# Post-norm chains with the reciprocal norm in PSUM, and squares summed by TensorE, in a two-layer decoder step

## The chip, the cores and the metric

The kernel runs on one core of one Trainium2 chip. The metric is the device time of one execution in microseconds (us). The median of three runs of the kernel before is 2349.43 us (2349.2 to 2352.71).

## The reference

One inference step of a two-layer trunk for a prompt of 1024 tokens and a group of 8 x 4 sample tokens, with shared weights and a model width of 1024. Layer 0 runs a convolution branch and a sliding-window attention branch behind one input projection; layer 1 is a gated linear recurrence. What bears on this change is what stands around each layer: the input is normed before the first projection, and the output of the last projection is normed (the post-norm), scaled and added to the layer's input.

```python
def rms_norm(x, g):
    xf = x.astype(jnp.float32)
    y = xf * lax.rsqrt(jnp.mean(xf * xf, axis=-1, keepdims=True) + NORM_EPS)
    return (y * g.astype(jnp.float32)).astype(x.dtype)

def even_layer(x, pos, conv_buf, kv_cache, pre_g, post_g, w_in, w_out, conv_w, conv_b, ln_g, ln_b):
    h = rms_norm(x, pre_g)
    proj = jnp.einsum('ntd,de->nte', h, w_in)
    ...
    y = jnp.einsum('nte,ed->ntd', jnp.concatenate([ya, yb], axis=-1), w_out)
    return x + rms_norm(y, post_g), conv_new, k, v

def odd_layer(x, s0, lb, pre_g, post_g, w_in, w_out, g_norm):
    h = rms_norm(x, pre_g)
    proj = jnp.einsum('ntd,de->nte', h, w_in)
    ...
    y = jnp.einsum('nte,ed->ntd', o, w_out)
    return x + rms_norm(y, post_g), s_new
```

So between the layers a token's 1024 values pass through two norms: the post-norm of layer 0, whose sum of squares is over `y`, and, once the sum `x + rms_norm(y)` is there, the pre-norm of layer 1, whose sum of squares is over that sum. The last output is the post-norm of layer 1 with its residual.

## The kernel before

Activations lie transposed: a tile has 128 features on the partitions and tokens along the free axis, so the width of 1024 is eight tiles, `k` or `ct` from 0 to 7. The 1056 tokens (1024 prompt and 32 sample) are cut in three chunks of `CW` = 384, 384 and 288 columns, chunk `c` = 0, 1, 2. A projection multiplies a 128 x 128 block of weights with such a tile. Weights and activations are each split in a high and a low fp32r part (for weights `w_high`, `w_split`: a ScalarE cast and a subtract on VectorE or GpSimd; for activations `self.xh`, `self.xl`), and three matmuls per tile stand for the full product, 24 for a chunk of eight tiles.

The order of work is not written out by hand. Jobs of TensorE (`dense`) run in a fixed order; everything else is a thread, a list of steps (`Atom`), each with an engine and the keys of the steps that it follows. While TensorE's matmuls are recorded, a planner with its own clock per engine (`sides`, `ready`, `account`) puts a step into its engine's queue when the planner's clock says that its inputs are there. The queues themselves run in order, with semaphores: a step that waits holds up whatever stands behind it on its engine. All operations are recorded by one helper, so every row of the profile has its line, L157; tiles tell them apart. `b` is any buffer in SBUF, `c` a buffer kept for the whole run (among them `xh` and `xl`, the ones matrix and the parameters), and `d`, `x`, `o` are tiles in PSUM: three, four and one of them.

The output projection of a layer (`project`) runs in three lists of jobs: `ja` with one half of the input features, for chunks 0 and 1, `jb` with the other half for the same chunks, and `jc` with both halves for chunk 2, eight jobs of 48 matmuls. As a tile of the result leaves PSUM, `ev_sum` squares it on ScalarE and adds the squares over the tiles on VectorE. Before `jb` starts, `post` spawns a thread for each chunk, which runs as follows:

- `stat` (TensorE, ScalarE): a matmul of the summed squares with a matrix of 1/128 (called the ones matrix here) gives the mean over the partitions in every row; `rstd_of` makes Ln and then Exp of it, which is the reciprocal norm. It is written to a half buffer in SBUF, `R[1]`.
- `ldx` (SyncE): the layer's input tile is loaded, `PX` = 3 tiles ahead (all eight for the last chunk of layer 1).
- `res` (VectorE): `y` times the post-norm's weight times `R[1]`, in place.
- `sum_` (GpSimd or VectorE, as the planner's clocks say): plus the input.
- In layer 0 then `hi` (ScalarE) and `lo` (VectorE), the high and low part of the next layer's input, `sq` (a store of the tile on SyncE, and its square on ScalarE) and `acc` (GpSimd or VectorE): the squares are added up over the tiles. In layer 1 `sq` is the store of the output alone.
- In layer 0 last `norm` (TensorE, ScalarE): the sum of squares times the ones matrix, and the reciprocal norm of layer 1's input, `R1`, by which the results of layer 1's projections are scaled as they leave PSUM.

The dense jobs of layer 1 use `xh` and `xl` of a chunk as soon as its `lo` steps are there. The first three jobs of layer 1 are cut by chunk (`HEAD0` = 3): three jobs on chunk 0, three on chunk 1, three on chunk 2, in 3 x 24 matmuls each. A matmul against the ones matrix is plain fp32 and appears as two records.

## Time and profile before

| what | value |
|---|---|
| median of three runs | 2349.43 us |
| the profiled execution | 2347.8 us, span 2344.8 us |
| TensorE (PE) busy | 2256.7 us, 96% |
| VectorE (DVE) busy | 1615.1 us, 69% |
| ScalarE (ACT) busy | 1023.7 us, 44% |
| GpSimd (POOL) busy | 1065.2 us, 45% |
| granted TensorE clock, mean | 0.987 of full |

The page's first part gives each engine's busy time; its second cuts the span in 40 slices, with TensorE's busy share and granted clock as digits (9 is 90% or more). The part of the trace that belongs to the change lies near the middle, at about 1120 to 1240 us, where layer 0 ends and layer 1 begins, and at the end, from about 2270 us. The busy tables by stretch show how much of each stretch an engine worked, and the granted clock in it; the timelines show single instructions and, in brackets, how long the engine had stood before them and who released it.

### The profile page before, as it was taken

To read this page: it belongs to the slowest core of one execution; us is meant where nothing else is said; L and a number is where in the kernel's file an instruction comes from. 1 tells how busy PE (TensorE), PEld (TensorE's weight loads), DVE (VectorE), ACT (ScalarE), POOL (GpSimd) and SP (SyncE) were. 2 spreads that over 40 slices of the span, in tenths; PEclk is the share of its full clock that TensorE was granted. 3 is DMA by queue.
4 is the path that set the end of the run, shared out by engine and by line. 5 is a ranking of instruction groups with operands and counts; after the bars stand their busy time and mean duration, and the time that the engine had idled before them with its cause. 6 is when DMAs were issued, how large, how long until landed. Compare 5 with 4: busy or idle time off the path is not lost.

```text
span 2344.8 us, 42760 instructions
## 1 busy us (share of the span) xinstructions
PE 2256.7 (96%) x17387; PEld 2115.6 (90%) x17387; DVE 1615.1 (69%) x2465; ACT 1023.7 (44%) x1856; POOL 1065.2 (45%) x706
## 2 busy tenths in 40 slices
PE   7999999999989999999979999999999999999997
PEld 6988888898887788899969999999999999998996
DVE  7999899998885656732776666666666666667336
ACT  5454454444445323332455444444454444444332
POOL 4655465555464523543654333333333333344436
PEclk9999999999999999999979999999999999999998
DMA  4131221221246978862540212222112221132535
GB/s 152 56 96 40 61 93 49 69 76 49 70 154 247 346 288 310 288 216 96 165 149 30 73 68 71 71 72 74 50 62 72 72 72 66 65 104 91 178 101 173
DMA packets 118173, 271.60 MB, mean 116 GB/s; under 512 B 32336, under 2 KB 59472, under 8 KB 117968
## 3 DMA queue, kind: packets, MB, share of 16 engines
q1 hardware_dynamic: 117968, 268.78, 33.5%
q8 instruction: 139, 2.28, 0.4%
q14 instruction: 66, 0.54, 0.1%
HBM read 215.00 MB, written 53.73 MB: 115 GB/s over the span
## 4 chain that ended last, share of the span: by engine, by line
PE 63%; DVE 3%; DMA 2%; ACT 1%; POOL 1%; issue 1%; SPq 0%; POOLq 0%; DVEq 0%; ACTq 0%
PE d L157 33%; PE x L157 29%; DVE b L157 3%; ACT b L157 1%; DMA b<-vc 1%; POOL b L157 1%; DVE c L157 1%; DMA b<-ybd 1%; PE o L157 0%; DMA b<-kc 0%; SPq L157 0%; DMA b<-x1d 0%; ACT c L157 0%; POOL c L157 0%; ACT L157 0%
## 5 line engine op out<-in xcount | busy, mean ns | idle before, releaser
L157 PE MATMUL d<-c,b 128*128 128x384 f32 (+1 forms) x7920 | 1393.2, 330 | 20.5 <-ACT b L157 8.6
L157 PEld LDWEIGHTS d<-c,b 128*128 128x128 f32 x7920 | 1284.2, 189 | 67.9 <-issue 40.3
L157 POOL TENSOR_TENSOR b<-b,b 128x1024 fp32r<-128x1024 f32 (+7 forms) x423 | 854.1, 2031 | 827.5 <-ACT b L157 616.6
L157 ACT ACTIVATE b<-b 128x384 f32<-128x384 f32 (+14 forms) x647 | 356.8, 567 | 801.6 <-DVE b L157 783.2
L157 PE MATMUL x<-c,b 128*128 128x384 f32 (+4 forms) x3616 | 581.3, 311 | 3.7 <-DVE b L157 2.9
L157 PEld LDWEIGHTS x<-c,b 128*128 128x128 f32 (+2 forms) x3616 | 540.0, 175 | 18.5 <-issue 5.1
L157 DVE SCALAR_TENSOR_TENSOR b<-b,c,b 128x1024 f32<-128x1024 f32 (+2 forms) x258 | 410.2, 1593 | 10.7 <-ACT b L157 8.3
L157 DVE TENSOR_TENSOR b<-b,b 128x384 f32<-128x384 f32 (+13 forms) x296 | 312.7, 1072 | 85.7 <-ACT b L157 69.9
L157 PE MATMUL x<-b,b 128*32 128x128 f32 (+12 forms) x4528 | 281.0, 340 | 12.2 <-POOL b L157 10.7
L157 DVE SCALAR_TENSOR_TENSOR b<-b,b 128x384 f32<-128x384 f32 (+3 forms) x216 | 193.2, 898 | 111.4 <-ACT b L157 103.2
L157 PEld LDWEIGHTS x<-b,b 64*32 64x32 f32 (+3 forms) x4528 | 201.0, 128 | 62.5 <-issue 38.0
L157 DVE TENSOR_TENSOR b<-d,b 128x384 f32<-128x384 f32 (+3 forms) x279 | 140.3, 509 | 142.4 <-PE d L157 133.8
L157 ACT CAST b<-b 128x1024 fp32r<-128x1024 f32 (+3 forms) x264 | 224.1, 862 | 31.8 <-DMA b<-od 7.8
L157 DVE TENSOR_TENSOR b<-x,b 128x384 f32<-128x384 f32 (+3 forms) x161 | 81.7, 508 | 130.7 <-PE x L157 115.8
L157 DVE COPY b<-x 128x512 f32<-128x512 f32 (+6 forms) x217 | 101.5, 479 | 77.3 <-PE x L157 70.1
L157 POOL TENSOR_SCALAR b<-b 128x32 f32<-128x32 f32 x40 | 28.6, 714 | 272.8 <-DVE b L157 272.8
L157 ACT COPY b<-x 128x512 f32<-128x512 f32 (+4 forms) x176 | 86.0, 496 | 143.7 <-PE x L157 132.1
L157 ACT COPY b<-d 32x384 f32<-32x384 f32 (+2 forms) x211 | 94.3, 447 | 123.4 <-DVE b L157 78.4
L157 DVE CUSTOM_DVE_ANT_0 b<-x,b 128x128 f32<-128x128 f32 (+8 forms) x144 | 72.0, 533 | 38.5 <-PE x L157 35.7
L157 ACT ACTIVATE b<-b,c 128x512 f32<-128x512 f32 (+1 forms) x112 | 95.1, 874 | 2.9 <-DVE b L157 0.5
L157 POOL COPY b<-b 128x32 f32<-128x32 f32 (+1 forms) x105 | 59.0, 571 | 50.3 <-DVE b L157 48.5
L157 POOL TENSOR_TENSOR b<-b,c 128x248 f32<-128x248 f32 (+1 forms) x48 | 66.8, 1408 | 23.5 <-PE d L157 16.3
(59 smaller groups left out, 928.4 us busy)
## 6 DMA issues: line engine op xcount, KB each, us to landing
b<-wc SPq DMA_DIRECT2D x64, 512.0 KB, 4.2
b<-wab SPq DMA_DIRECT2D x56, 512.0 KB, 5.9
b<-kc SPq DMA_DIRECT2D x64, 448.0 KB, 6.5
b<-vc SPq DMA_DIRECT2D x64, 448.0 KB, 7.5
b<-woa SPq DMA_DIRECT2D x32, 512.0 KB, 4.3
b<-woc SPq DMA_DIRECT2D x32, 512.0 KB, 4.1
b<-yd SPq DMA_DIRECT2D x16, 528.0 KB, 6.4
ybd<-b SPq DMA_DIRECT2D x16, 512.0 KB, 3.0
```

The source lines that it names most:

```text
L157: r = f(*a, **k)
```

## The change

The reciprocal norm `R[1]` of the post-norm is written to the one PSUM tile `o` in place of a half buffer in SBUF, in both layers, so `res` reads one operand from SBUF and one from PSUM. Since there is one `o` tile, the statistic of chunk 1 or 2 gets a further condition: the last `res` of the chunk before.

In layer 0, for chunks 1 and 2 (`BYPE`), the step `acc` goes. TensorE sums over the partitions and over the tiles at once: `norm(0)` multiplies the squares of tiles 0 to 3 with the ones matrix into one PSUM tile, and ScalarE copies the result to a half buffer; `norm(1)` does tiles 4 to 7 into another, VectorE adds the two, and `rstd_of` follows. Chunk 0 keeps the adds and its single matmul (`norm1`). The claim of half buffers that must be free before a chunk's first load goes from `n + 4` to `n + 6`, and `R1` is taken before the three threads are spawned and no longer in chunk 0's last step.

```diff
--- before.py
+++ after.py
@@ -48,6 +48,7 @@
 PTAPS = 5
 QUEUE = 800
 HOLE = 700
+BYPE = (1,2)
 LAT = dict(pe=54.0, dve=33.0, act=33.0, pool=78.0)
 OVER = dict(dve=83.0, act=95.0, pool=54.0)
 
@@ -1619,7 +1620,7 @@
                 if two:
                     nc.tensor.matmul(p[:, :w], self.ones.f, self.last[:, :w], start=False, stop=True)
                     self.last.free()
-                R[key] = A.alloc(384)
+                R[key] = self.po()
                 self.rstd_of(R[key][:, :w], p[:, :w])
                 ss.free()
             return f
@@ -1639,8 +1640,6 @@
                 else:
                     nc.vector.scalar_tensor_tensor(y, y, self.P(P_POST, L * 8 + k), R[1][:, :w],
                                                    op0=OP.mult, op1=OP.mult)
-                if k == KT - 1:
-                    R[1].free()
             return f
 
         def sum_(k):
@@ -1683,22 +1682,37 @@
                     t.free()
             return f
 
-        def norm():
-            if c == 0:
-                self.R1 = A.alloc(NTOK)
+        def norm1():
             p = self.px()
             nc.tensor.matmul(p[:, :w], self.ones.f, R["ss2"][:, :w], start=True, stop=True)
             self.rstd_of(self.R1[:, cs], p[:, :w])
             R["ss2"].free()
 
+        def norm(half):
+            def f():
+                p = self.px()
+                for k in range(4 * half, 4 * half + 4):
+                    nc.tensor.matmul(p[:, :w], self.ones.f, R["t", k][:, :w], start=(k % 4 == 0), stop=(k % 4 == 3))
+                    R["t", k].free()
+                if half == 0:
+                    R["s"] = A.alloc(384)
+                    nc.scalar.copy(R["s"][:, :w], p[:, :w])
+                    return
+                s = R["s"][:, :w]
+                nc.vector.tensor_tensor(s, p[:, :w], s, op=OP.add)
+                self.rstd_of(self.R1[:, cs], s)
+                R["s"].free()
+            return f
+
         tag = ("post", L, c)
         K = lambda n, k: (tag, n, k)
         xs = [Atom(ldx(k), "sp", [("sum", L, c, 3)], K("x", k)) for k in range(KT)]
         n = PX if (L, c) != (1, 2) else KT
-        xs[0].claim = (0, n + 4)
+        xs[0].claim = (0, n + 6)
         atoms, xs = xs[:n], xs[n:]
-        atoms.append(Atom(stat(1), "pe", [("sum", L, c, KT - 1)], K("st", 1)))
-        fs = ([("dve", res), ("pool", sum_), ("act", hi), ("dve", lo), ("act", sq), ("dve", acc)] if L == 0 else
+        atoms.append(Atom(stat(1), "pe", [("sum", L, c, KT - 1)] + ([(("post", L, c - 1), 0, KT - 1)] if c else []),
+                          K("st", 1)))
+        fs = ([("dve", res), ("pool", sum_), ("act", hi), ("dve", lo), ("act", sq)] + [("dve", acc)] * (c not in BYPE) if L == 0 else
               [("dve", res), ("pool", sum_), ("sp", sq)])
         n = len(fs)
         for slot in range(KT + n - 1):
@@ -1711,8 +1725,11 @@
                     atoms.append(Atom(fs[st][1](k), fs[st][0], d, K(st, k)))
                     if st == 1 and xs:
                         atoms.append(xs.pop(0))
+                    if (L, st, k) == (0, 4, 3) and c in BYPE:
+                        atoms.append(Atom(norm(0), "pe", [K(4, 3)]))
         if L == 0:
-            atoms.append(Atom(norm, "pe", [K(5, KT - 1)], ("r1", c), (1, 0) if c == 0 else None))
+            atoms.append(Atom(norm(1), "pe", [K(4, KT - 1)], ("r1", c)) if c in BYPE else
+                         Atom(norm1, "pe", [K(5, KT - 1)], ("r1", c)))
         self.spawn(f"post{L}{c}", 0.01 * c, atoms, None, ("y", L, c))
 
 
@@ -2437,6 +2454,8 @@
             self.until(("ods", 1))
             for b in [self.cmask, self.rmask, self.qz] + self.smp1:
                 b.free()
+        if L == 0:
+            self.R1 = self.A.alloc(NTOK)
         for c in range(3):
             self.post(L, c)
         self.dense(jb)
```

The planner moves instructions in the two layers' ends and nowhere else. On TensorE, at the start of layer 1, before: two ones matmuls (the norm of chunk 0 from the sum `b1178`, the statistic of chunk 2 from `b1161`) within the first job on chunk 0, `d_12639`. `c4`, `c5`, `c12`, `c13` are `xh` and `xl` tiles, `c19` is the ones matrix, and `b1215`, `b1216` are the parts of the weights.

```order
L157 MATMUL d_12639<-c12_82,b1215_12539 128x384
L157 MATMUL d_12639<-c4_74,b1216_12540 128x384
L157 MATMUL x_12678<-b1178_12214,c19_89 128x384
L157 MATMUL x_12689<-b1161_12087,c19_89 128x288
L157 MATMUL d_12639<-c5_75,b1215_12539 128x384
L157 MATMUL d_12639<-c13_83,b1215_12539 128x384
L157 MATMUL d_12639<-c5_75,b1216_12540 128x384
```

After, the norm of chunk 0 and the statistic of chunk 1 stand in the first job on chunk 0; three jobs follow, and between them and the first job on chunk 1, `d_12802`, come the four squares of the first half of chunk 1:

```order
L158 MATMUL d_12712<-c8_78,b1227_12634 128x384
L158 MATMUL x_12776<-b1237_12732,c19_89 128x384
L158 MATMUL x_12776<-b1239_12750,c19_89 128x384
L158 MATMUL x_12776<-b1243_12767,c19_89 128x384
L158 MATMUL x_12776<-b1244_12774,c19_89 128x384
L158 MATMUL d_12802<-c1_71,b1212_12540 128x384
L158 MATMUL d_12802<-c9_79,b1212_12540 128x384
L158 MATMUL d_12802<-c1_71,b1213_12541 128x384
L158 MATMUL d_12802<-c2_72,b1212_12540 128x384
L158 MATMUL d_12802<-c10_80,b1212_12540 128x384
L158 MATMUL d_12802<-c2_72,b1213_12541 128x384
L158 MATMUL x_12812<-b1246_12788,c19_89 128x384
```

So the first ones matmul is followed by three more and by six matmuls of the job, and then by the second half, `x_12812`. Chunk 2's two halves stand in the same way, the first within the last job on chunk 1, the second within the first job on chunk 2. ScalarE's copy of the first half-sum stands in its queue before the `hi` steps of chunk 1's tiles 5 to 7, and likewise for chunk 2.

On VectorE, at the same place, before: the last steps of chunk 0 (`lo` into `c15` and `c16`, the adds of squares into `b1178`) between steps of chunk 1, whose `R[1]` is `b1156`.

```order
L157 TENSOR_SCALAR c20_90<-c17_87 128x1
L157 SCALAR_TENSOR_TENSOR b1049_10990<-b1049_10990,c17_87,b1156_12050 128x384
L157 SCALAR_TENSOR_TENSOR c9_79<-b1018_10701,c17_87,c1_71 128x384
L157 TENSOR_TENSOR b1178_12214<-b1178_12214,b1220_12582 128x384
L157 SCALAR_TENSOR_TENSOR c15_85<-b1099_11366,c17_87,c7_77 128x384
L157 SCALAR_TENSOR_TENSOR b1055_11108<-b1055_11108,c17_87,b1156_12050 128x384
L157 SCALAR_TENSOR_TENSOR c10_80<-b1035_10845,c17_87,c2_72 128x384
L157 SCALAR_TENSOR_TENSOR c16_86<-b1101_11396,c17_87,c8_78 128x384
L157 TENSOR_TENSOR b1178_12214<-b1178_12214,b1229_12650 128x384
L157 TENSOR_TENSOR b1227_12644<-b1217_12565,b1226_12643 128x1024
L157 SCALAR_TENSOR_TENSOR b1074_11211<-b1074_11211,c17_87,b1156_12050 128x384
L157 SCALAR_TENSOR_TENSOR c11_81<-b1049_10990,c17_87,c3_73 128x384
```

After: the two last adds of squares of chunk 0 (into `b1163`) stand before the evacuation of the eighth tile of chunk 2 (the copy from `d_12531`), and no step of chunk 1 stands in front of them.

```order
L158 SCALAR_TENSOR_TENSOR c16_86<-b1101_11396,c17_87,c8_78 128x384
L158 COPY b1099_11366<-d_12455 128x288
L158 TENSOR_TENSOR b1158_12079<-b1158_12079,b1210_12527 128x288
L158 TENSOR_TENSOR b1163_12114<-b1163_12114,b1207_12499 128x384
L158 TENSOR_TENSOR b1163_12114<-b1163_12114,b1214_12564 128x384
L158 COPY b1101_11396<-d_12531 128x288
L158 TENSOR_TENSOR b1158_12079<-b1158_12079,b1218_12597 128x288
```

What moved: all of chunk 1's steps went behind the layer-1 constants, and chunk 0's before them.

On VectorE at the end of layer 1, before: the last multiply of chunk 1 (by `b2144`) behind the evacuation of the eighth tile of chunk 2, `d_23398`.

```order
L157 TENSOR_TENSOR b2048_22046<-b2193_23308,b2048_22046 128x384
L157 SCALAR_TENSOR_TENSOR b2060_22133<-b2060_22133,c17_87,b2144_22925 128x384
L157 SCALAR_TENSOR_TENSOR b2087_22247<-b2087_22247,c17_87,b2144_22925 128x384
L157 TENSOR_SCALAR b2089_22277<-d_23398,c17_87 128x288
L157 SCALAR_TENSOR_TENSOR b2089_22277<-b2089_22277,c17_87,b2144_22925 128x384
L157 TENSOR_TENSOR b2005_21589<-b2005_21589,b2209_23490 128x288
L157 TENSOR_TENSOR b2012_21676<-b2012_21676,b2209_23490 128x288
```

After: the last multiply of chunk 1 (by `o_23273`) before the evacuation of the seventh tile, `x_23346`.

```order
L158 SCALAR_TENSOR_TENSOR b2059_22141<-b2059_22141,c17_87,o_23273 128x384
L158 SCALAR_TENSOR_TENSOR b2086_22255<-b2086_22255,c17_87,o_23273 128x384
L158 TENSOR_TENSOR b2086_22255<-b2194_23373,b2086_22255 128x384
L158 SCALAR_TENSOR_TENSOR b2088_22285<-b2088_22285,c17_87,o_23273 128x384
L158 TENSOR_SCALAR b2086_22255<-x_23346,c17_87 128x288
L158 TENSOR_TENSOR b2150_22980<-b2150_22980,b2196_23420 128x288
L158 TENSOR_SCALAR b2088_22285<-d_23425,c17_87 128x288
L158 TENSOR_TENSOR b2004_21597<-b2004_21597,o_23498 128x288
L158 TENSOR_TENSOR b2011_21684<-b2011_21684,o_23498 128x288
```

What moved: chunk 1's chain ends one job of chunk 2 earlier, and with it the stores of chunk 1, which stand on SyncE in front of the eight loads for chunk 2 in both kernels.

## Rows read from the trace of the kernel before

**Rows 1.** The page: busy share of TensorE, and its granted clock in 40 slices.
```profile
PE 2256.7 (96%) x17387; PEld 2115.6 (90%) x17387; DVE 1615.1 (69%) x2465; ACT 1023.7 (44%) x1856; POOL 1065.2 (45%) x706
PEclk9999999999999999999979999999999999999998
```
**Rows 2.** Busy table, seam: length, PE, PEld, DVE, ACT, POOL; clock, DMA share, GB/s.
```profile
1178.44:1238.06 59.62, 43.11 (x227) 40.86 (x225) 39.93 (x69) 33.80 (x60) 27.38 (x27) 0.80 0.38 126
...
1180.00:1190.00 10.00, 0.71 (x5) 0.39 (x3) 9.46 (x21) 4.45 (x9) 5.82 (x6) 0.63 0.84 283
1190.00:1200.00 10.00, 9.81 (x37) 8.92 (x38) 5.66 (x11) 5.00 (x11) 0.00 (x0) 0.68 0.27 88
...
1210.00:1220.00 10.00, 5.97 (x17) 5.36 (x18) 6.17 (x10) 4.50 (x8) 4.71 (x5) 0.50 0.26 83
```
**Rows 3.** Timeline of TensorE at the seam: start, us, work, [idle before, releaser].
```profile
1178.44 2.27 PE L157 MATMUL d<-c,b 128*128 128x384 f32 x12
1190.19 2.61 PE L157 MATMUL x<-b,c 128*128 128x384 f32 x4 [9.47 <-DVE b L157]
1192.18 4.37 PE L157 MATMUL d<-c,b 128*128 128x384 f32 x12
...
1214.03 1.65 PE L157 MATMUL x<-b,c 128*128 128x384 f32 x2 [7.04 <-DVE b L157]
1214.91 4.62 PE L157 MATMUL d<-c,b 128*128 128x384 f32 x12
...
1238.06 7.26 PE L157 MATMUL d<-c,b 128*128 128x384 f32 x41
```
**Rows 4.** Chain that ended last, two stretches of the output projection: start, us, work.
```profile
1113.15 4.16 PE x L157 x24
...
1146.81 6.33 PE x L157 x48
```
**Rows 5.** Timeline of TensorE, three ones matmuls in a row at full clock.
```profile
717.51 1.94 PE L157 MATMUL x<-b,c 128*128 128x384 f32 x6
719.38 0.66 PE L157 MATMUL o<-b,b 128*64 128x128 f32 x8
```
**Rows 6.** Instructions by shape, 1120 to 1245: busy us, mean ns; idle before.
```profile
L157 POOL TENSOR_TENSOR b<-b,b 128x384 f32<-128x384 f32 x21 | 28.3, 1358 | 20.5 <-DVE b L157 18.6 <-ACT b L157 1.8
L157 DVE SCALAR_TENSOR_TENSOR b<-b,c,b 128x384 f32<-128x384 f32 x16 | 20.8, 1305 | 1.1 <-ACT b L157 1.1
L157 ACT ACTIVATE b<-b 128x384 f32<-128x384 f32 x27 | 13.6, 518 | 13.4 <-DVE b L157 13.2
L157 ACT ACT_TABLE_LOAD x6 | 7.7, 1283 | 0.1
L157 DVE TENSOR_TENSOR b<-d,b 128x384 f32<-128x384 f32 x6 | 3.3, 552 | 12.0 <-PE d L157 12.0
```
**Rows 7.** Timeline of VectorE at the seam.
```profile
1182.93 0.61 DVE L157 SCALAR_TENSOR_TENSOR b<-b,c,b 128x384 f32<-128x384 f32 x1
...
1197.13 0.55 DVE L157 TENSOR_TENSOR b<-b,b 128x384 f32<-128x384 f32 x1
...
1211.94 1.57 DVE L157 SCALAR_TENSOR_TENSOR c<-b,c,c 128x288 fp32r<-128x288 f32 x2
```
**Rows 8.** Busy table of TensorE alone, in layer 0: length, busy, clock, DMA, GB/s.
```profile
973.60:977.00 3.40, 0.88 (x3) 1.00 0.83 306
977.00:980.40 3.40, 3.40 (x17) 0.63 0.02 7
```
**Rows 9.** Timeline of all engines at the kernel's end.
```profile
2328.50 1.77 DVE L157 TENSOR_TENSOR b<-b,b 128x288 f32<-128x288 f32 x3 [0.35 <-ACT b L157]
2329.63 3.76 SPq L157 DMA_DIRECT2D b<-x1d  x8
...
2333.66 4.23 DVE L157 TENSOR_TENSOR b<-b,b 128x288 f32<-128x288 f32 x8 [3.38 <-DMA b<-x1d]
...
2337.96 0.79 POOL L157 TENSOR_TENSOR b<-b,b 128x288 f32<-128x288 f32 x1 [0.76 <-DVE b L157]
```

## The prediction

> **What bounds the kernel now.** I read the page first, then the busy table of the seam between the two layers, then TensorE's timeline there, then the instructions by shape, and last the timeline of the kernel's end. TensorE is busy for 96% of the span and its clock row is at nine tenths or more nearly everywhere [rows 1], so a change can pay only where TensorE stands or runs slowly, or behind its last matmul. The seam is the largest such place. From the first matmul of layer 1 at 1178.44 to the first one after its chunk-by-chunk jobs at 1238.06 lie 59.62 us, of which TensorE is busy for 43.11, at a mean clock of 0.80 [rows 2, 3]. It stands twice, 9.47 and 7.04 us, each time at a matmul against the ones tile and each time released by VectorE [rows 3]: the first is the next norm of chunk 0, the second that of chunk 1, and both wait for the sum of squares that VectorE and GpSimd add up tile by tile.
>
> The other loss is the clock. [...] Check of the sum: the seam's matmuls need six times 24 at 384 columns, 0.1733 each (4.16 for 24), and three times 24 at 288 columns, 0.132 each (6.33 for 48) [rows 4], 34.5 us; plus four against the ones tile, which at full clock are 0.64 us for 384 columns and at three quarters of that, 0.49, for 288: six records, that is three matmuls of 384, 384 and 288 columns, stand from 717.51 to 719.38 [rows 5], 1.87 us where these two prices give 1.77. That makes 2 x 0.64 + 2 x 0.49 = 2.3, in all 36.8. The waits are 16.5, so 59.6 - 36.8 - 16.5 = 6.3 us went to the clock. What can be won at the seam is 22.8 us.
>
> Behind the last matmul the end of the kernel is a chain: the last chunk's reciprocal norm is there when VectorE starts at 2328.50, three multiplies run, and then VectorE stands 3.38 us for the layer-1 inputs, whose eight loads SyncE issues only from 2329.63, behind the stores of chunk 1. The last add ends at 2338.75 [rows 9].
>
> **The change part by part.** *Norm of chunk 0 at the seam.* It keeps its adding chain, but chunk 1's norm now starts only after all of chunk 0's multiplies, so VectorE no longer does chunk 1's work between chunk 0's. In the order its last two adds of squares stand before the evacuation of the eighth tile, where before the last stood behind the layer-1 constants and eight steps of chunk 1 or 0. Multiplies that read the reciprocal norm from PSUM also keep one SBUF input only: with two, 384 columns take 1305 ns in the mean, while an add with one input in PSUM takes 552 [rows 6] and a free VectorE multiply 0.61 [rows 7]. I take this wait, 9.47 us, as gone, and its half-clock stretch with it. The cover that makes it cheap is the eight third-chunk jobs in front; if they don't cover it, up to 9.5 us stay.
>
> *Norm of chunk 1.* Its first statistic moves from the middle of the third-chunk jobs to the first layer-1 job, 21 matmuls in (3.64 us); with the two ones matmuls TensorE is at 4.9 us after the seam's start. Nothing of chunk 1 is done by then: its whole chain now stands at the seam. ScalarE does four Ln and Exp steps, about 0.55 each (518 ns for plain ones [rows 6]), so the first multiply ends at 7.2. After that a tile needs a GpSimd add (1358 ns in the mean, collisions counted) and a VectorE subtract with two SBUF inputs (0.61 alone): between 1.36, side by side, and 1.97, in turn. The row that this resembles is GpSimd's own mean, which has such turns in it already; I take 1.6. Add k ends at 8.2 + 1.6k, its square 1.1 later on ScalarE: number 3 at 14.1, number 7 at 20.5, and up to 2.3 later because a table load (1283 ns [rows 6]), a tanh and the copy of the first half-sum stand in ScalarE's queue between: 22.9. TensorE: 51 dense matmuls after 4.9 bring it to 13.8, four ones matmuls to 16.3, six dense to 17.4, four more to 19.9 if nothing waits. The last one must follow square 7: 23.5. So a wait of 3.6 us, in pieces between ones matmuls. What is queued behind it: the other 18 matmuls of the chunk-1 job, and chunk 2's statistic.
>
> *Norm of chunk 2.* Nine dense and the statistic take TensorE to 25.6, 51 dense to 34.4. The chain at 288 columns runs at three quarters, 1.2 us a tile from about 27, so its first four squares are there. Half 0 ends at 36.4; six and six dense to 38.2. But ScalarE holds the copy of half 0 ahead of the last tiles' work and cannot do it before 36.4; copy, three scales, four squares, table load and tanh, 5.5 us, put the last square at 41.9, the last ones matmul at 42.4 instead of 40.2: a wait of 2.2. Then 66 dense at 288 columns, 8.7: 51.1 us.
>
> The added matmuls are fourteen ones matmuls more, 7 x 0.64 + 7 x 0.49 = 7.9 us on the engine that bounds the kernel; they are in this sum, about 45.3 without any wait. The 14 adds that they replace were not on TensorE's path except through the two waits. The seam's gain is 59.6 - 51.1 = 8.5 us. Its bounds: 14.3 if neither chain waits, and 2.5 if the clock falls in both norm stretches (3 us each, as it cost before). A sum of waits of this size can do that: with TensorE busy for 0.88 us of the 3.4 at 973.60 the next 3.4 us were granted 0.63 [rows 8]. I take it as not falling, since the ones matmuls run between the pieces, and no piece is worked out above 2 us.
>
> What an operand in PSUM costs VectorE and ScalarE has one row to bound it: the add with one input in PSUM takes 552 ns, an SBUF add without a collision 0.55 us [rows 6, 7]. So I price it at nothing, with 0.1 us either way for each of the sixteen multiplies. [...]
>
> *The bigger claim and the earlier layer-1 page.* Loads of the residual now ask for two more half buffers before they start, and one page is taken before the third-chunk jobs. Weight prefetch could run thinner for it; Before, the third-chunk jobs run at full pace (48 matmuls in 6.33 us [rows 4]), so I price this at 0, at worst one wait of 2 us, about one of GpSimd's weight splits.
>
> *The end.* In layer 1 VectorE's last multiply of chunk 1 stood behind the evacuation of the eighth tile; now it stands before that of the seventh, some 6 us earlier (one third-chunk job of 48 matmuls, 6.33 us). So chunk 1's stores, and behind them the eight loads, go out about that much earlier, and the 3.38 us are gone. Eight multiplies from PSUM and four adds are left on VectorE, 12 x 0.45 to 0.53, 5.4 to 6.4 us from 2328.5, so the last add ends near 2334.7 instead of 2338.75: 4 us. Bounds: 1.5 (loads still late, the multiplies alone shorter) and 5.
>
> **Sum.** 8.5 + 4 = 12.5 us. The profiled execution took 2347.8 us (span 2344.8), so 2335.3; the median of the runs, 2349.43, lies 1.6 above that execution, so 2337.
>
> **The rivals.** *Nothing waits* (GpSimd and VectorE side by side, under 1.36 a tile): gain 14.3 + 5 = 19.3, 2330. For it, the free multiply of 0.61; against it, ScalarE's own order at the half-sum copy. *The clock falls twice and the loads stay late*: 2.5 + 1.5 = 4, 2345, no change that counts. For it, the row at 973.60. *PSUM does not free the multiplies* (the change doesn't do what it says): each stays at 1.3, 0.7 more a tile, 5.6 us on chunk 1's chain and 1 on chunk 2's: gain 6, 2343. Against it, the 552 ns. *Slower*: the chunk-1 chain, now alone at the seam, keeps the pace it had. Its third multiply started at 1182.93 and its last subtract ended near 1213.5 [rows 7], six tiles in 30.6 us, 5.1 each. Then square 7 comes at 50.3 and the last ones matmul at 50.9, 31 us after it was due at 19.9; chunk 2 at 3.8 a tile ends at 86 where 67.6 was due, 18 more. Seam 45.3 + 49 = 94, 35 slower, less 4: 2380. It decides from 3.2 us a tile, where chunk 1's wait grows by 12.5. Against it: that pace was made by chunk 0's steps and evacuations in the same queue, which are no longer there.
>
> **How the numbers follow.** A measurement of this kernel tells about 0.2%, 4.7 us, from no change. Forecast (gain 6 to 17) 0.58, nothing waits 0.12, PSUM frees nothing 0.10, clock and loads 0.13, slower 0.07. Faster: the first three and 0.02 of the fourth, 0.82; same 0.11; slower 0.07. The range runs from the second case, 2330, to the fourth, 2345, which leaves out the slow one and the edges.
>
> **What would show it.** After: TensorE's wait for chunk 0's norm gone; the seam about 51 us from its first layer-1 matmul; waits only in front of ones matmuls, released by ScalarE, no more than some 6 us in all; the granted clock near 1 through it; multiplies reading `o` at about 0.6 us; VectorE not waiting for `x1d` loads at the end. Wrong would be a single wait above 4 us at either half-sum, a clock of 0.5 to 0.7 in the seam, or a VectorE wait of 3 us for loads after the last matmul.

## The result, and the profile after

The changed kernel takes 2337.72 us in the median of five runs (2334.24 to 2338.5), the kernel before 2349.43 us (2348.23 to 2352.71): a ratio of 0.9948, 95% interval [0.9937, 0.9959], some 12 us faster. The profiled execution took 2337.72 us, with a span of 2335.9 us.

The page of the changed kernel, the rows that answer to [rows 1]:

```profile
PE 2264.7 (97%) x17415; PEld 2121.1 (91%) x17415; DVE 1601.3 (69%) x2469; ACT 1024.3 (44%) x1858; POOL 1042.8 (45%) x690
PEclk9999999999999999999999999999999999999998
```

The busy table of the seam in the changed kernel, from the first matmul of layer 1 to the first one behind the nine cut jobs, with the columns of [rows 2]:

```profile
1179.25:1229.51 50.26, 47.32 (x257) 41.30 (x255) 30.28 (x64) 35.06 (x62) 18.35 (x18) 1.00 0.46 150
1180.00:1190.00 10.00, 10.00 (x56) 9.47 (x55) 7.72 (x22) 5.16 (x10) 1.01 (x1) 1.00 0.50 177
1190.00:1200.00 10.00, 8.61 (x36) 5.91 (x35) 8.88 (x15) 7.32 (x14) 7.45 (x6) 1.00 0.40 138
1210.00:1220.00 10.00, 8.47 (x44) 7.13 (x43) 5.39 (x12) 6.45 (x14) 3.60 (x4) 1.00 0.43 144
```

The seam is 50.26 us long where it was 59.62, and the granted clock is 1.00 in every slice, where three slices of before show 0.63, 0.68 and 0.50 [rows 2].

TensorE's timeline there, against [rows 3]:

```profile
1182.90 1.45 PE L158 MATMUL x<-b,c 128*128 128x384 f32 x4
1183.90 9.36 PE L158 MATMUL d<-c,b 128*128 128x384 f32 x51
1193.10 1.45 PE L158 MATMUL x<-b,c 128*128 128x384 f32 x4
1195.49 1.83 PE L158 MATMUL x<-b,c 128*128 128x384 f32 x4 [0.94 <-ACT b L158]
1196.87 1.51 PE L158 MATMUL d<-c,b 128*128 128x384 f32 x6
1198.82 3.39 PE L158 MATMUL x<-b,c 128*128 128x384 f32 x8 [0.45 <-ACT b L158]
...
1213.01 2.10 PE L158 MATMUL x<-b,c 128*128 128x288 f32 x8
1214.73 2.21 PE L158 MATMUL d<-c,b 128*128 128x384 f32 x12
1216.78 0.65 PE L158 MATMUL x<-b,c 128*128 128x288 f32 x2
1218.96 2.00 PE L158 MATMUL x<-b,c 128*128 128x288 f32 x6 [1.53 <-ACT b L158]
```

The row at 1182.90 is the norm of chunk 0 and the statistic of chunk 1: it waits for nothing, where chunk 0's norm waited 9.47 us. The halves of chunk 1 stand at 1193.10 and 1198.82, those of chunk 2 at 1213.01 and 1216.78, with three short waits, 2.92 us in all, each released by a square of ScalarE.

The end of the kernel, timeline of VectorE and SyncE, against [rows 9]:

```profile
2318.60 3.76 SPq L158 DMA_DIRECT2D b<-x1d  x8
2322.80 0.82 DVE L158 TENSOR_TENSOR b<-b,o 128x288 f32<-128x288 f32 x2 [1.23 <-ACT o L158]
...
2328.29 0.78 DVE L158 TENSOR_TENSOR b<-b,b 128x288 f32<-128x288 f32 x1
```

The eight loads go out 4.2 us before VectorE's first multiply, not 1.1 behind it, and no wait for them is left. From that multiply to the end of the last add it is 6.3 us (2322.80 to 2329.07) where it was 10.25 (2328.50 to 2338.75).

The profiled pair adds up so: the seam begins 0.8 us later, is 9.4 shorter; from its end to the last chunk's ones matmuls the changed kernel takes 1090.9 us against 1087.9, 2.9 longer; the end is 4.0 shorter, and 0.8 us more lie behind the last add: in all the 8.9 us between the spans. About half of the 2.9 (30 us at a clock lower by 0.05 are 1.5 us, as an estimate) is a lower clock in a place where the programs are alike, one row of the busy table of TensorE each (length, busy, clock, DMA, GB/s), before and after:

```profile
2108.00:2138.00 30.00, 25.79 (x166) 0.94 0.33 104
```

```profile
2100.00:2130.00 30.00, 25.79 (x161) 0.89 0.33 109
```

The five runs of the changed kernel lie 4 us apart, the fastest (2334.24 us) at a mean clock of 0.994 and the slowest (2338.5) at 0.989, so the medians, 11.7 us apart, are the better measure of the change.

### The profile page after: what moved, and what is told of

Read it like the earlier page. It is cut to its first block, busy times and chain, and to the rows that moved or that the text cites. A ratio compares the mean times of both kernels' runs of the same rounds, so it can differ in the third digit from the quotient of the medians.

```text
span 2335.9 us, 42808 instructions
## 1 busy us (share of the span) xinstructions
PE 2264.7 (97%) x17415; PEld 2121.1 (91%) x17415; DVE 1601.3 (69%) x2469; ACT 1024.3 (44%) x1858; POOL 1042.8 (45%) x690
## 4 chain that ended last, share of the span: by engine, by line
PE 59%; issue 3%; DVE 2%; POOL 2%; ACT 1%; DMA 0%; SPq 0%; POOLq 0%; ACTq 0%; DVEq 0%
PE d L158 31%; PE x L158 27%; DVE b L158 2%; POOL b L158 2%; ACT b L158 1%; DMA b<-x 0%; DMA b<-woa 0%; ACT c L158 0%; ACT L158 0%; SPq L158 0%; POOL c L158 0%; DVE c L158 0%; ACT o L158 0%; POOLq L158 0%; DVE b L2147 0%
## 5 line engine op out<-in xcount | busy, mean ns | idle before, releaser
L158 POOL TENSOR_TENSOR b<-b,b 128x1024 fp32r<-128x1024 f32 (+7 forms) x407 | 835.2, 2064 | 832.0 <-ACT b L158 605.5
L158 PE MATMUL x<-c,b 128*128 128x384 f32 (+3 forms) x3616 | 578.9, 311 | 3.3 <-DVE b L158 2.9
L158 PEld LDWEIGHTS x<-c,b 128*128 128x128 f32 (+1 forms) x3616 | 539.5, 175 | 16.9 <-issue 5.0
L158 DVE TENSOR_TENSOR b<-b,b 128x384 f32<-128x384 f32 (+14 forms) x290 | 320.3, 1118 | 82.5 <-ACT b L158 67.4
L158 DVE SCALAR_TENSOR_TENSOR b<-b,c,b 128x1024 f32<-128x1024 f32 (+1 forms) x218 | 362.1, 1661 | 6.9 <-ACT b L158 4.5
L158 PE MATMUL x<-b,b 128*32 128x128 f32 (+12 forms) x4552 | 284.6, 341 | 12.5 <-POOL b L158 11.6
L158 ACT COPY b<-x 128x512 f32<-128x512 f32 (+5 forms) x178 | 86.9, 496 | 149.6 <-PE x L158 137.9
L158 ACT ACTIVATE b<-b,c 128x512 f32<-128x512 f32 (+2 forms) x114 | 96.3, 869 | 3.3 <-DVE b L158 1.2
```

The lines of the kernel that those rows point to most:

```text
L158: r = f(*a, **k)
```

## The experiments

Each was timed against the kernel before on its own chip, but not all on one chip: e1 to e4, e5 to e8, e9 to e11 and e12 stand on four, where the kernel before has medians of 2348.61, 2348.49, 2348.40 and 2346.53 us. Between runs of different chips the ratio to before is the safer measure; 0.001 of it is 2.3 us. The seam is measured as above, in the profiled execution of each. In the two marked *, statistics or squares of a chunk stand in front of it, and its length does not compare exactly; in the kernel before the statistic of chunk 1 does so too, one ones matmul of 0.64 us (two records; the four at 1182.90 in the changed kernel start 0.32 us apart).

| run | what differs | seam, us | median, us | ratio to before |
|---|---|---|---|---|
| before | | 59.62 | 2349.43 | 1 |
| changed | | 50.26 | 2337.72 | 0.9948 [0.9937, 0.9959] |
| e1 | claim and page only | 71.29 | 2361.86 | 1.0062 [1.0048, 1.0076] |
| e2 | PSUM, no squares on TensorE | 57.03 | 2346.75 | 0.9994 [0.9985, 1.0003] |
| e3 | squares, no PSUM | 62.04 | 2351.52 | 1.0009 [1.0000, 1.0018] |
| e12 | e3's order, operand in PSUM | 59.45 | 2349.03 | 1.0007 [0.9998, 1.0016] |
| e5 | changed order, operand in SBUF, five small buffers | 52.78 | 2345.02 | 0.9984 [0.9976, 0.9993] |
| e9 | changed, five small buffers | 50.30 | 2341.41 | 0.9966 [0.9954, 0.9977] |
| e10 | changed, claim n + 4 | 53.24* | 2338.94 | 0.9961 [0.9949, 0.9973] |
| e11 | PSUM in layer 0 only | 50.26 | 2339.67 | 0.9967 [0.9954, 0.9980] |
| e4 | changed, one PSUM group | 48.24 | 2333.38 | 0.9938 [0.9925, 0.9951] |
| e6 | e4, squares in fp32r | 47.49 | 2334.66 | 0.9937 [0.9925, 0.9950] |
| e7 | e4, half of the squares added | 52.56 | 2340.25 | 0.9966 [0.9953, 0.9979] |
| e8 | e4, chunk 0 too | 44.23* | 2336.31 | 0.9950 [0.9938, 0.9962] |

**e1: the claim and the earlier page alone** (against the kernel before)

```diff
-        xs[0].claim = (0, n + 4)
+        xs[0].claim = (0, n + 6)
...
-            if c == 0:
-                self.R1 = A.alloc(NTOK)
...
+        if L == 0:
+            self.R1 = self.A.alloc(NTOK)
```

> The kernel before with the bigger claim (n + 6) and the earlier page for R1 alone: the reciprocal norm stays in SBUF, all squares are added by VectorE and GpSimd. The planner then already puts chunk 1's chain behind chunk 0's. Theory A (the gain needs all three: the order, the PSUM operand and the squares on TensorE; each alone gives part): chunk 0's wait falls from 9.5 to about 4 us, chunk 1's stays near 7 because its chain still has two SBUF operands per multiply and the adds; some 4 us faster than before, 2345, with a half-clock stretch left. Rival B (the PSUM operand alone does it): no change, 2349. Rival C (the order alone does it): 2338, seam near 51 us.

It is 13 us slower, which no theory had. TensorE's timeline of this run:

```profile
1185.05 2.93 PE L158 MATMUL x<-b,c 128*128 128x384 f32 x4 [6.08 <-DVE b L158]
...
1215.48 1.65 PE L158 MATMUL x<-b,c 128*128 128x384 f32 x2 [8.59 <-DVE b L158]
...
1237.09 1.33 PE L158 MATMUL x<-b,c 128*128 128x288 f32 x2 [6.75 <-DVE b L158]
```

With the claim and the earlier page, which this run does not tell apart, the planner puts chunk 1's chain behind chunk 0's. Chunk 0's wait falls from 9.47 to 6.08 us, but the whole chain of chunk 1 now stands at the seam at its old pace, and chunk 2's behind it: 8.59 and 6.75 us, and a mean clock of 0.78 over the seam. So the order by itself is a loss; the other two parts have to pay for it first.

**e2 and e3: one of the two other parts each** (against the changed kernel)

```diff
-BYPE = (1,2)
+BYPE = ()
```

> The changed kernel with BYPE empty: reciprocal norm in PSUM and the order kept, but chunks 1 and 2 add their squares on VectorE and GpSimd again, one ones matmul each. Theory A: TensorE is spared 7.9 us of ones matmuls, but comes to chunk 1's norm about 5 us earlier, while the sum of squares is one or two adds later; the seam gets one wait of 6 to 9 us with a half-clock stretch behind it and a smaller one for chunk 2: 2342, 4 us slower than the change. Rival B (PSUM operand alone does it): 2337, like the change. Rival C (order alone): 2338.

```diff
-                R[key] = self.po()
+                R[key] = A.alloc(384)
...
+                if k == KT - 1:
+                    R[1].free()
```

> The changed kernel with the reciprocal norm in a half buffer in SBUF; squares on TensorE, the bigger claim and the condition on the statistic are kept. Theory A: the multiplies of chunks 1 and 2 go from 0.6 to about 1.3 us beside GpSimd's adds, the chain of chunk 1 is 5.6 us later at its last square, the seam 5 us longer, and at the end the multiplies collide again: 2343 to 2344. Rival B: 2349, all of the gain gone. Rival C (order alone): 2338, no change from the changed kernel.

TensorE's timelines, first e2, then e3:

```profile
1181.02 1.45 PE L158 MATMUL x<-b,c 128*128 128x384 f32 x4
...
1203.33 1.65 PE L158 MATMUL x<-b,c 128*128 128x384 f32 x2 [7.89 <-DVE b L158]
...
1224.19 1.33 PE L158 MATMUL x<-b,c 128*128 128x288 f32 x2 [5.47 <-DVE b L158]
```

```profile
1187.44 2.93 PE L158 MATMUL x<-b,c 128*128 128x384 f32 x4 [6.07 <-DVE b L158]
...
1203.75 1.83 PE L158 MATMUL x<-b,c 128*128 128x384 f32 x4 [1.48 <-ACT b L158]
1206.92 0.91 PE L158 MATMUL x<-b,c 128*128 128x384 f32 x2 [1.34 <-ACT b L158]
```

The parts divide by chunk. With the reciprocal norm in PSUM, and the order that the planner then makes, chunk 0's wait is gone (e2); without it 6 us stay (e1, e3). With the squares on TensorE the waits of chunks 1 and 2, 7.89 and 5.47 us, become short pieces (e3, changed). Against e1 the first part gives 15.1 us, the second 10.3, both together 24.1: they nearly add up, and neither alone is faster than the kernel before by more than the measurement tells. Theory A held in kind, but its prices for a missing part, 4 and 6 us, were half of the 9.0 and 13.8 found. C falls with e1, B with e2.

**e5, e9 and e12: the operand, or the order that comes with it?** The planner's cost rule lets a VectorE step collide with GpSimd's when more than one of its operands lies in SBUF (`two`), so e3 has another order than the changed kernel. e5 keeps the changed order and moves the operand; to make room it gives up three small buffers, and e9 is its control. Some neighbours changed places in e5 all the same: at the seam 54 dense matmuls stand between the statistic of chunk 2 and its first half-sum, in the changed kernel 51. e12 keeps e3's order on every engine and has the operand in PSUM; the planner is made to reckon as in e3 (`lie`), and a half buffer is taken as in e3 (`R["h"]`).

```diff
-                R[key] = self.po()
+                R[key] = self.rfix
...
-        two = sum(x.space != bass.MemoryType.PSUM for x in ins) > 1
+        two = sum(x.space != bass.MemoryType.PSUM for x in ins) > (2 if self.lie else 1)
...
+        self.rfix = A.fixed(384)
```

> The changed kernel with every engine's order kept as it is (one pair of ScalarE steps swapped), but the reciprocal norm in a buffer of its own in SBUF in place of the PSUM tile, and three small buffers fewer to make room. So only the place of one operand differs. Theory A (the PSUM operand keeps the multiplies from colliding with GpSimd's adds): multiplies of 384 columns 1.2 to 1.4 us in place of 0.60, each chain 0.7 us a tile slower, waits back before chunk 0's norm and the halves of chunk 1, seam 58 to 62 in place of 50.3 us, the end's multiplies collide too: 2348 to 2352. Rival E (what helped is the order that the planner makes when it holds the port for free): 2338 to 2340, seam within 2 us of 50.3.

```diff
-    BUFS = {"page": 28, "half": 17, "small": 8}
+    BUFS = {"page": 28, "half": 17, "small": 5}
```

> The changed kernel with five small buffers in place of eight and nothing else: the control for the run with the same order and the reciprocal norm in SBUF, which also gave up three small buffers and lost some 4 us in layer 1, away from the change. Theory A2 (the operand alone costs what that run lost at the seam and the end, 3 us, and the buffers the rest): 2341 to 2342. Rival (the buffers cost nothing and the operand costs all 7.3 us): 2337.7.

```diff
+                R[key] = self.po()
+                R["h"] = A.alloc(384)
...
-        two = sum(x.space != bass.MemoryType.PSUM for x in ins) > 1
+        two = sum(self.lie or x.space != bass.MemoryType.PSUM for x in ins) > 1
```

> The kernel of the run with squares on TensorE and the reciprocal norm in SBUF, with every engine's order exactly kept, but the reciprocal norm in PSUM: the planner is made to reckon as if it were in SBUF. Theory A2 (the operand itself is worth some 3.6 us in either order, the rest of the 13.8 us between that run and the changed kernel is the order in front of the seam): 2348, with a wait of 4 to 6 us before chunk 0's norm still there, multiplies of 384 columns near 0.60 us. Rival B2 (the operand does most of it, whatever the order): 2339 to 2341, chunk 0's wait under 2 us.

The multiplies by shape, 1120 to 1245 us, of the changed kernel, of e5 and of e12:

```profile
L158 DVE SCALAR_TENSOR_TENSOR b<-b,c,o 128x384 f32<-128x384 f32 x16 | 9.6, 603 | 0.2 <-ACT o L158 0.2
```

```profile
L158 DVE SCALAR_TENSOR_TENSOR b<-b,c,c 128x384 f32<-128x384 f32 x16 | 17.7, 1114 | 0.0
```

```profile
L158 DVE SCALAR_TENSOR_TENSOR b<-b,c,o 128x384 f32<-128x384 f32 x16 | 9.6, 605 | 0.0
```

The operand makes the multiplies short, 603 ns in place of 1114 to 1356 (1305 in [rows 6]). But e5 already spoke against theory A: its seam is 52.78 us and not 58 to 62, and rival E was nearer. Theory A2 was formed from that, and the seams of the two other runs bear it out: with the order held the operand is worth 2.6 us of seam (e3 to e12) or 2.5 us (e9 to e5), and the order 9.2 us (e12 to changed). In the time of the whole kernel the operand's part is less sure: 2.5 us by medians but 0.5 by ratios from e3 to e12, which lies within the noise, and 3.6 or 4.2 us from e9 to e5; the order's part is 11.3 or 13.9 us. What the order does is seen on VectorE in front of the seam, first in e12, whose layer 1 starts at 1174.71, then in the changed kernel, where it starts at 1179.25:

```profile
1175.35 0.46 DVE L158 COPY b<-d 128x288 f32<-128x288 f32 x1 [0.32 <-ACT b L158]
...
1178.47 0.55 DVE L158 TENSOR_TENSOR b<-b,b 128x384 f32<-128x384 f32 x1
...
1181.70 1.69 DVE L158 TENSOR_TENSOR b<-b,b 128x384 f32<-128x384 f32 x2 [0.88 <-POOL b L158]
```

```profile
1174.90 5.67 DVE L158 TENSOR_TENSOR b<-b,b 128x288 f32<-128x288 f32 x3
1180.49 0.45 DVE L158 COPY b<-d 128x288 f32<-128x288 f32 x1
```

In the changed kernel chunk 0's last two adds of squares are two of the three at 1174.90, ahead of the eighth evacuation, and end 1.3 us after the seam's start. In e12 VectorE's last two stand behind the constants of layer 1, at 1178.47 and first of the two at 1181.70; between them GpSimd does two more, and VectorE waits 0.88 us for the second. TensorE waits for the last:

```profile
1182.31 2.92 PE L158 MATMUL x<-b,c 128*128 128x384 f32 x4 [5.35 <-DVE b L158]
```

Rival B2 falls with e12, and E holds for the larger part. What makes the planner's order is not told apart further: e12 differs from the changed kernel in the reckoning of the costs and in the half buffer that it takes, both as in e3. E9 also shows what the three buffers cost, 3.7 us by medians (4.2 by ratios, the intervals just overlapping), none of it in the seam (50.30).

**e10: the claim back at n + 4** (against the changed kernel)

```diff
-        xs[0].claim = (0, n + 6)
+        xs[0].claim = (0, n + 4)
```

> The changed kernel with the claim back at n + 4. The condition on the statistic stays, so chunk 1's multiplies still follow chunk 0's, but chunk 0's loads and steps stand later in the order: its last add of squares is behind the layer-1 constants again, and one multiply of chunk 1 ahead of them. Theory A2 (the order in front of the seam decides): chunk 0's norm waits 2 to 4 us again, 2340 to 2342. Rival J (the claim is of no use once the reciprocal norm is in PSUM): 2337 to 2338.

TensorE's timeline of this run, at the norm of chunk 0, the last squares of chunk 1 and the end of the seam:

```profile
1184.52 0.91 PE L158 MATMUL x<-b,c 128*128 128x384 f32 x2 [0.78 <-DVE b L158]
...
1199.67 0.91 PE L158 MATMUL x<-b,c 128*128 128x384 f32 x2 [1.79 <-ACT b L158]
1202.82 4.21 PE L158 MATMUL x<-b,c 128*128 128x384 f32 x6 [2.23 <-ACT b L158]
...
1229.42 3.34 PE L158 MATMUL d<-c,b 128*128 128x288 f32 x24
1232.60 4.36 PE L158 MATMUL x<-c,b 128*128 128x384 f32 x24
```

The row at 1229.42 is the last of the nine cut jobs, so the seam runs from 1179.36 to 1232.60, 53.24 us, 3.0 longer than the changed kernel's. The run is 1.2 us slower by the medians and 3.1 by the ratios, with overlapping intervals; that lies between rival J and A2 and decides neither. The mechanism is not A2's: with one add of chunk 0 behind the constants its norm waits 0.78 us, not 2 to 4. The longer part is chunk 1's second half, whose waits of 1.79 and 2.23 us stand where the changed kernel has 0.45. So the claim still gives some 3 us of seam with both other parts in place.

**e11: layer 1 as before** (against the changed kernel)

```diff
-                R[key] = self.po()
+                R[key] = self.po() if L == 0 else A.alloc(384)
...
-        atoms.append(Atom(stat(1), "pe", [("sum", L, c, KT - 1)] + ([(("post", L, c - 1), 0, KT - 1)] if c else []),
+        atoms.append(Atom(stat(1), "pe", [("sum", L, c, KT - 1)] + ([(("post", L, c - 1), 0, KT - 1)] if c and L == 0 else []),
```

> The changed kernel with the reciprocal norm in PSUM in layer 0 only; in layer 1 it is in a half buffer in SBUF again, without the condition between the chunks. Theory A2 (the end's 4 us come with layer 1's part of the change): VectorE waits 3 to 4 us for the layer-1 inputs behind the last matmul again, 10.3 us from the last chunk's reciprocal norm to the last add in place of 6.3; 4 us slower than the change, 2341 to 2342, seam unchanged at about 50. Rival K (the end is shorter because the third chunk starts earlier, whatever layer 1 does): 2337.7.

The end in this run:

```profile
2318.54 2.41 DVE L158 TENSOR_TENSOR b<-b,b 128x288 f32<-128x288 f32 x3 [0.29 <-ACT b L158]
2324.64 4.29 DVE L158 TENSOR_TENSOR b<-b,b 128x288 f32<-128x288 f32 x8 [3.69 <-DMA b<-x1d]
```

The wait for the loads is back, 3.69 us, and from the first multiply to the last add it is 10.4 us: 4.1 more, as A2 said; the seam is 50.26 as before the edit. The whole kernel is 2.0 us slower by medians and 4.5 by ratios, with a spread of 5 us between its runs and overlapping intervals, so the end's 4.1 us are shown by the trace and not by the time. In e5 the same stretch is 6.9 us and in e12 8.8, with a wait of 3.46 for the loads: at the end, too, the order does most.

**e4: eight ones matmuls in one PSUM tile** (against the changed kernel)

```diff
-                p = self.px()
+                p = R["p"] if half else self.px()
...
-                    nc.tensor.matmul(p[:, :w], self.ones.f, R["t", k][:, :w], start=(k % 4 == 0), stop=(k % 4 == 3))
+                    nc.tensor.matmul(p[:, :w], self.ones.f, R["t", k][:, :w], start=(k == 0), stop=(k == 7))
...
-                    R["s"] = A.alloc(384)
-                    nc.scalar.copy(R["s"][:, :w], p[:, :w])
+                    R["p"] = p
                     return
-                s = R["s"][:, :w]
-                nc.vector.tensor_tensor(s, p[:, :w], s, op=OP.add)
-                self.rstd_of(self.R1[:, cs], s)
+                self.rstd_of(self.R1[:, cs], p[:, :w])
```

> The changed kernel with the eight ones matmuls of a norm accumulated in one PSUM tile: no ScalarE copy of the first half-sum, no VectorE add, the reciprocal norm read from PSUM. Theory A (the copy stands in ScalarE's queue ahead of the casts and squares of tiles 5 to 7 and makes the waits before the second halves): the waits before the second halves, 1.5 us for chunk 2, go, 1 to 2 us faster than the change, 2336. Rival D (the pace of the tile chain sets these waits, the copy hides beside it): same within 0.5 us, 2337.5.

In the changed kernel ScalarE stands for the copy of half 0 of chunk 2, in front of the last tiles' casts and squares:

```profile
1215.14 0.40 ACT L158 COPY b<-x 128x288 f32<-128x288 f32 x1 [3.40 <-PE x L158]
```

In e4 TensorE's timeline has no wait in chunk 2:

```profile
1208.61 2.10 PE L158 MATMUL x<-b,c 128*128 128x288 f32 x8
1210.34 1.93 PE L158 MATMUL d<-c,b 128*128 128x384 f32 x9
1212.11 1.36 PE L158 MATMUL x<-c,b 128*128 128x288 f32 x9
1213.30 2.11 PE L158 MATMUL x<-b,c 128*128 128x288 f32 x8
```

The planner also put chunk 2's second half later, behind 18 dense matmuls instead of 12, but that is not what frees it: without the copy ScalarE's last square of chunk 2 ends by 1211.6, 36.2 us after the seam's start and before even twelve would be done, where in the changed kernel ScalarE still casts and squares at 1218.5, 39.2 us after it. The seam is 2.0 us shorter, and the kernel 2.3 us faster by ratios (0.9938 and 0.9948, intervals overlapping) and 4.3 by medians. Theory A for chunk 2; in chunk 1 waits of 0.94, 0.37 and 0.36 us stay, so there D holds. e4 has the lowest median of all fourteen kernels.

**e6, e7, e8: what do the added matmuls cost?** (against e4) e6 rounds the squares of chunks 1 and 2 to fp32r.

```diff
-                    R["t", k] = A.alloc(384)
+                    R["t", k] = A.alloc(384, c in BYPE)
...
-                    nc.scalar.activation(R["t", k][:, :w], y, AF.Square)
+                    nc.scalar.activation(t.r[:, :w] if c in BYPE else t[:, :w], y, AF.Square)
...
-                    nc.tensor.matmul(p[:, :w], self.ones.f, R["t", k][:, :w], start=(k == 0), stop=(k == 7))
+                    nc.tensor.matmul(p[:, :w], self.ones.r, R["t", k].r[:, :w], start=(k == 0), stop=(k == 7))
```

> The one-group kernel with the squares of chunks 1 and 2 written in fp32r, so that the sixteen ones matmuls run in one pass: 0.17 and 0.13 us in place of 0.64 and 0.49, 6.6 us less TensorE work. Theory A (chunk 1 is paced by its tiles, chunk 2 is not): in chunk 1 the saved time turns into longer waits for the last squares, all but about 0.5 us, in chunk 2 most of its 2.9 us is gained: 3 to 4 us faster than one group, 2330. Rival F (TensorE's sum alone decides): 6.6 us faster, 2327. Rival G (chunk 2 waits as well): 1 us, 2332.

e7 has VectorE and GpSimd add the first four squares of a chunk again.

```diff
-                for k in range(4 * half, 4 * half + 4):
-                    nc.tensor.matmul(p[:, :w], self.ones.f, R["t", k][:, :w], start=(k == 0), stop=(k == 7))
+                if half == 0:
+                    nc.tensor.matmul(p[:, :w], self.ones.f, R["t", 0][:, :w], start=True, stop=False)
...
+                for k in range(4, 8) if half else ():
+                    nc.tensor.matmul(p[:, :w], self.ones.f, R["t", k][:, :w], start=False, stop=(k == 7))
...
-        fs = ([("dve", res), ("pool", sum_), ("act", hi), ("dve", lo), ("act", sq)] + [("dve", acc)] * (c not in BYPE) if L == 0 else
+        fs = ([("dve", res), ("pool", sum_), ("act", hi), ("dve", lo), ("act", sq)] + [("dve", acc)] if L == 0 else
...
+                    if not (L == 0 and st == 5 and c in BYPE and k > 3):
```

> The one-group kernel, in which the squares of tiles 0 to 3 of chunks 1 and 2 are added by VectorE or GpSimd and go through one ones matmul; only tiles 4 to 7 go to TensorE one by one: three ones matmuls fewer a chunk, 1.9 and 1.5 us. Theory A (VectorE paces the chain, its additions collide at about 1.5 us): three additions in chunk 1's chain put its last square 3 to 4 us later, half of it covered: 1 to 3 us slower than one group, 2335. Rival F (TensorE's sum alone decides): 3.4 us faster, 2330.

e8 sends the squares of chunk 0 to TensorE too.

```diff
-BYPE = (1,2)
+BYPE = (0,1,2)
```

> The one-group kernel with chunk 0 included (BYPE = (0, 1, 2)): seven more ones matmuls of 0.64 us. Theory A (chunk 0's norm waits for nothing any more, so its adds are free): 4.5 us slower than one group, 2338. Rival H (the seven adds held up VectorE and GpSimd, and chunk 1's chain starts and runs earlier without them): no change, 2333, or faster.

The busy table of the seam, e4 first, then e6:

```profile
1175.33:1223.57 48.24, 46.57 (x256) 41.48 (x255) 29.91 (x62) 34.68 (x60) 18.68 (x18) 1.00 0.47 156
```

```profile
1179.34:1226.83 47.49, 42.96 (x240) 40.11 (x239) 29.82 (x62) 34.56 (x60) 18.69 (x18) 0.93 0.49 158
```

TensorE is busy 3.6 us less in e6, with 240 records in place of 256, one for each of the sixteen ones matmuls in fp32r, but the seam is only 0.75 us shorter: the time turned into waits (1.89, 0.48, 0.59 and 0.58 us in chunk 1, 0.98 in chunk 2) and a clock of 0.93. The time is no better (ratios 0.9937 and 0.9938): rival G is the nearest. E7 has the additions back in the chain and a wait for them:

```profile
1197.13 1.65 PE L158 MATMUL x<-b,c 128*128 128x384 f32 x2 [6.93 <-DVE b L158]
```

Three ones matmuls a chunk less, and 6.9 us slower than e4 (6.6 by ratios), more than theory A had. E8, whose norm of chunk 0 gains nothing, is 2.9 us slower than e4, of 4.5 expected. TensorE is busy for all 44.23 us of its seam, so the waits of e4, 1.67 us in chunk 1, are gone as H's reason has it, and 4.5 less 1.67 is 2.8. But its lower end, 2333.96, lies within e4's runs, so between A and H it decides only loosely.

## Why the prediction was right

**The sum.** Forecast 2337, measured 2337.72; seam 8.5 forecast and 9.4 found, end 4 and 4.0. That the medians agree within 1 us is partly chance: in the profiled pair the seam and the end give 13.4 us, of 12.5 forecast, and 4.5 us are lost elsewhere, about 1.5 of them to the clock, so that the profiled execution took 2337.72 us where 2335.3 were forecast. The steps on chunks 1 and 2, on the operand and on the end stood on the right mechanism, the one on chunk 0 on an incomplete one, and the claim was not worth nothing.

**Chunk 0's norm.** The wait went, as the step said, and the stretch behind it in which twelve dense matmuls took 4.37 us [rows 3]: the busy table of before gives a clock of 0.51 from 1192.2 to 1196.4, the changed kernel has 1.00 in every slice of the seam, and its 51 dense matmuls at 1183.90 take 9.36 us. The step's reason was incomplete. It named three things: chunk 1's steps no longer stand between chunk 0's, the last two adds of squares stand ahead of the eighth evacuation, and multiplies with an operand in PSUM are short (603 ns). The first alone (e1, with the earlier page) leaves 6.08 us and lengthens the seam by 11.7; the first and the third together, in e3's order (e12), leave 5.35. So the place of chunk 0's last steps is needed. It is not a matter of the constants alone, since one add behind them costs 0.78 us (e10): in e12 four of the seven adds come only after them, two of these on GpSimd. The step took this order from the listing and did not say that it comes with the operand, by way of the planner.

**Chunk 1's norm.** The pace of 1.6 us a tile was near: add 7 was due 19.4 us after the seam's start, and GpSimd's last three adds end at 20.0:

```profile
1195.71 3.55 POOL L158 TENSOR_TENSOR b<-b,b 128x384 f32<-128x384 f32 x3 [1.52 <-DVE b L158]
```

The last ones matmul of the chunk was due at 23.5 and was over at 22.5, when the dense matmuls go on at 1201.75.

**Chunk 2's norm.** Forecast 2.2 us of wait because of the copy, found 1.53, and e4 shows that it was the copy. For both chunks the sum had 5.8 us of waits on top of 45.3 without any (the seam gets fifteen more ones matmuls and not fourteen, since chunk 1's statistic moves into it). By the same working the changed kernel has 50.26 - 45.3 = 5.0, of which the timeline shows 2.92 as standing; the rest is spread over rows such as the four ones matmuls at 1198.82, 3.39 us where 2.56 were priced.

**The added matmuls.** 7.9 us were charged to TensorE's sum. As a count that is right, but e6 shows that the sixteen ones matmuls of squares, made cheaper by 6.6 us as priced (TensorE is busy for 3.6 us less), shorten the seam by 0.75: chunk 1 waits for its last squares anyway, and chunk 2 begins to. So most of their price lies in time in which TensorE would have waited, and the additions that they replace are the dear part (e7).

**An operand in PSUM at nothing.** Right: 603 ns at 384 columns against 0.61 us for a free multiply from SBUF [rows 7]. What the multiplies gain is 603 ns against 1114 in the one order and 605 against 1356 in the other (e12, e3). With both operands in SBUF, two multiplies of the kernel before differ with what GpSimd did: the one at 1176.21 took 2.75 us while GpSimd was at work, the one at 1182.93 took 0.61 us [rows 7] while GpSimd stood:

```profile
1167.45 11.10 POOL L157 TENSOR_TENSOR b<-b,b 128x1024 fp32r<-128x1024 f32 x5 [1.79 <-issue]
...
1176.21 2.75 DVE L157 SCALAR_TENSOR_TENSOR b<-b,c,b 128x384 f32<-128x384 f32 x1
...
1183.62 1.30 POOL L157 TENSOR_TENSOR b<-b,b 128x384 f32<-128x384 f32 x1 [3.25 <-DVE b L157]
```

In the changed kernel the multiplies at 1190.66 and 1191.96 lie within three adds of GpSimd (3.90 us from 1190.29) and take 0.60 us each.

**The claim at nothing.** Not right, though the sum did not suffer. The prediction looked for thinner weight prefetch; what the claim does is set the order of the chains. By itself, with the earlier page, that is 13 us of loss (e1); with the faster chains it gives some 3 us of seam (e10), a gain that the time of the kernel does not show clear of noise. The rival that went slower, a chunk-1 chain alone at the seam at its old pace, is what e1 shows, at 71 us of seam and not 94.

**The end.** Right, by the earlier stores and loads (e11), with 0.6 us of it from the operand (e5). Against VectorE's first multiply the loads go out 5.3 us earlier than before, of some 6 forecast.

**The clock.** No stretch below full in the seam, as taken: 1.00 in every slice, with waits of 2.92 us in all.

## What to carry to other kernels

Where a planner sets the order, a cheaper operand acts twice, by its own time and by what the planner then moves ahead; hold the order fixed to tell the two apart, since here the order was worth 9 us of the seam and the operand 2.5. A reordering is not good or bad in itself: putting one chain behind another cost 13 us while the chains were slow and gave some 3 us of the seam once they were short, so parts of such a change have to be tried in pairs. Here a matmul that took an addition out of a chain was priced by the chain that TensorE waits for, not by its own time.

## What the runs showed of the hardware beyond that

Less TensorE work went with a lower clock: e6 has 3.6 us less to do in the seam than e4 and stands 4.5 us in it instead of 1.67, and it was granted 0.93 in place of 1.00 (one profiled execution each). A VectorE multiply of 384 columns that reads one operand from PSUM ran at a mean of 603 to 605 ns in the seven kernels where it was read by shape (changed, e2, e4, e6, e7, e8, e12), with GpSimd at work in the same stretch; with both operands in SBUF its mean lay at 1114 to 1356 ns (e5, before, e1 and e3).
